# RWKV-7 keys stage: a slab's blocks and bonus sums written inside the next slab's projection, four small copies a slab on ScalarE

## The chip, the cores and the metric

The kernel runs on one core of a Trainium2 chip. The metric is the device time of one launch in microseconds (us). The engines of the core are TensorE (PE in the profile, its weight loads PEld), VectorE (DVE), ScalarE (ACT), GpSimd (POOL) and SyncE (SP), which here issues the DMAs. The engines run their own instruction lists in order and wait for one another by semaphores.

## What is computed

One inference step of two decoder layers, an RWKV-7 layer and a native sparse attention layer, for 512 prompt tokens and 8 sequences of 4 sample tokens. The change is in the RWKV-7 layer. Cut to what matters, the reference computes there:

```
r, k, v, z = einsum(stack([xr, xk, xv, xg]), w_rkvz)
a = sigmoid(a0 + (xa @ a1) @ a2)
kk = heads(k * k_k);  kk = kk / max(sqrt(sum(kk * kk, -1)), 1e-12)
k = k * (1 + (a - 1) * k_a)
y, S = wkv_scan(S0, r, decay, k, v, -kk, kk * a)
bonus = (sum(r * k * r_k, -1) * v)
```

The scan is done in chunks of 64 tokens. For each chunk and head the kernel needs the strictly lower (nilpotent) 64 x 64 block of products between the vectors kk * a and -kk, scaled by the decay, and later its inverse. The bonus needs one sum a head and token of r * k * r_k.

## The kernel before

The 544 tokens (512 of the prompt, 32 of the samples) lie along the free dimension in two halves of 272 columns (256 prompt tokens and 16 sample columns each); the 1024 channels are eight slabs of 128 partitions, two heads a slab. A projection of a slab (products, L317) is eight steps over the input channels, each of three products (high x high, high x low, low x high parts) for two halves: 48 matmuls at L325. Its result lies in a PSUM tile of tag pp.

The stage around the change is keys (L914). For each slab m from 0 to 7 it loads and splits the weights, projects the keys (L964; in the profile "pp<-t"), and then makes the scaled vectors: squares and a copy of k on ScalarE (L966, L968); the cumulated decay (L973, VectorE) and its exponentials (L979, L980, ScalarE); the sums a head of the squares (head_sums, L953, into PSUM tags s0 and s1) with L987, L989 and L990 on ScalarE behind them; the normalised kk (L992 to L995, VectorE and ScalarE); k2 (L998, VectorE) and b = kk * a (L1000, GpSimd); and the tiles ar (L1005, L1007 on VectorE) and bk (L1006 on GpSimd, L1008 on VectorE), which go to DRAM by four DMAs of SP.

Then come the two steps that the change moves. n_blocks (L927) takes a PSUM tile of tag pr, fills it with 16 matmuls of 64 x 64 blocks (L932; the profile shows 32 entries), masks it into NTt[m] on VectorE (L935) and sends it to DRAM by four DMAs (L940). The bonus part multiplies r, r_k and k2 into rk (L1016, VectorE), sums it a head in two halves (head_sums again, L953, each half in a tile of tag pr) and copies each half to bss on ScalarE (L1022). The tag pr has two buffers, the tag bs three, and the tiles upx, upi, ukkn, uar and ubk one each.

Between them stand three small copies of sample columns, 128 x 32 each, on GpSimd: of kkn, b and k2 into arS and bkS (L1017 to L1019). A fourth, of the sigmoid of the decay into sgS, stands at L971. All four go through the helper samp (L463), whose GpSimd copy is L468 and whose ScalarE copy is L466.

At the end of a slab after(m) (L615) does some steps of the inversion of the first four slabs' blocks (IV: 4, 6 and 6 steps after slabs 4, 5 and 6) and projects values (VS: one slab after each of slabs 2 to 6, three after slab 7; in the profile "pp<-x", with L608 and L612 behind it). value(m) uses bss[m].

The program order is not the order on the engines. The framework's scheduler makes each engine's list: it plays the program through with a model of the instructions' times and takes, of those that the model holds ready, the one that stands first in the program. A tile gets its buffer in the same play. The block tc.issue_after(x) adds an edge that keeps each instruction written in it behind x on the engine of x.

Of the kernel before, what the change touches and what calls it, by code (L numbers as in the profile page):

```python
# [11 lines left out]
AF = mybir.ActivationFunctionType  # L12
# [6 lines left out]
KT = 8  # L19
NT = 544  # L20
HN = 272
HP = 256
# [201 lines left out]
class K:  # L224
# [152 lines left out]
    @staticmethod  # L377
    def h2(t):
        return t.rearrange("p (h n) -> p h n", h=2)
# [534 lines left out]
    def keys(self, Xk, R, out, SG, AA, NTt, PC, arS, bkS, sgS, samp, dAR, dBK, ND, after):  # L914

        nc, I, h2 = self.nc, self.I, self.h2
        ident, gmask = self.C("ident"), self.C("gmask")
        WE = self.WE
        omk = self.c0("omk", (128, 8))
        sums = self.sums.bitcast(F32)  # L920
        reset = self.t("rst")
        nc.sync.dma_start(reset, I["reset"])
        nc.vector.tensor_scalar(omk, self.vec[:, VI["ka"]], -1.0, 1.0, op0=OP.mult, op1=OP.add)
        nkk = self.c0("nkk", (128, 8))
        nc.vector.tensor_scalar(nkk, self.vec[:, VI["kk"]], -1.0, None, op0=OP.mult)

        def n_blocks(p, ar, bk):  # L927
            g, i = divmod(p, 4)
            pw = self.t("pr", (128, 8, 64))
            for c in range(8):  # L930
                for r, par in PARS:
                    nc.tensor.matmul(pw[r, c, :], bk[r, 1, c, :], ar[r, c, 0, :],  # L932
                                     start=True, stop=True)
            t = NTt[p]
            nc.vector.tensor_tensor(t, pw, gmask[:, None, 0:64].to_broadcast([128, 8, 64]), OP.mult)  # L935
            for par in range(2):
                for b in range(2):
                    r = slice(par * 64 + b * 32, par * 64 + b * 32 + 32)
                    j = b * 64 + par * 32 + i * 8
                    nc.sync.dma_start(ND[g][j:j + 8].rearrange("c s t -> s c t"), t[r, :, b * 32:b * 32 + 32])  # L940

        def chunks(t):
            return t.rearrange("p (h c) n -> p h c n", h=2)

        def pv(t):
            return h2(t)[:, :, :HP].rearrange("p h (c n) -> p h c n", c=4)

        def head_sums(x, tags):

            out = []  # L950
            for h in range(2):
                ps = self.t(tags[h], (128, 512))
                nc.tensor.matmul(ps[:, :HN], sums, x[:, h * HN:(h + 1) * HN], start=True, stop=True)  # L953
                out.append(ps)
            return out

        for m in range(KT):
            g, i = divmod(m, 4)
            NTt.append(self.t("p", (128, 8, 64)))
            if PLAN["TN"]:  # L960

                nc.gpsimd.memset(NTt[m][:, 0, 0:1], 0.0)
            w = self.weight(I["rkvz"][1, m], 128, WE["WK"][m])
            pt = self.project(w, Xk)  # L964
            sq = self.t("d")
            nc.scalar.activation(h2(sq), pt[:, :, :HN], AF.Square, scale=self.V("kk", m))  # L966
            kr = self.t("d")
            nc.scalar.activation(h2(kr), pt[:, :, :HN], AF.Copy)  # L968

            sg, aa = SG[m], AA[m]  # L970
            samp(sgS[:, m], h2(sg)[:, :, HP:HN], nc.gpsimd)  # L971
            cs = sg
            nc.vector.tensor_tensor_scan(cs, reset, sg, 0.0, OP.mult, OP.add)  # L973
            csv = pv(cs)
            px = self.t("upx", (128, 8, 65))
            nc.gpsimd.memset(px[:, :, 0:1], 1.0)
            pi = self.t("upi", (128, 8, 64))
            with self.tc.issue_after(self.loaded.ins):
                nc.scalar.activation(chunks(px)[:, :, :, 1:65], csv, AF.Exp, scale=-DEC)  # L979
                nc.scalar.activation(chunks(pi), csv, AF.Exp, scale=DEC)  # L980
            nc.gpsimd.tensor_copy(PC[:, m], px[:, :, 64])


            ln = self.t("d")
            s2 = sq
            for h, ps in enumerate(head_sums(sq, ("s0", "s1"))):
                nc.scalar.activation(h2(s2)[:, h], ps[:, :HN], AF.Relu, bias=self.C("nfloor"))  # L987
            with self.tc.issue_after(self.loaded.ins):
                nc.scalar.activation(ln, s2, AF.Ln, scale=float(2 ** 20), bias=self.C("floor"))  # L989
            nc.scalar.activation(ln, ln, AF.Exp, scale=-0.5, bias=self.C("l2"))  # L990
            kkn = self.t("ukkn")
            nc.vector.scalar_tensor_tensor(kkn, kr, nkk[:, m:m + 1], ln, op0=OP.mult, op1=OP.mult)  # L992
            nc.scalar.activation(ln, ln, AF.Square, scale=math.sqrt(0.5))
            nc.vector.scalar_tensor_tensor(ln, s2, 1e-24, ln, op0=OP.add, op1=OP.mult)
            nc.vector.scalar_tensor_tensor(kkn, ln, 1.5, kkn, op0=OP.subtract, op1=OP.mult)  # L995
            nc.scalar.activation(cs, aa, AF.Identity, scale=self.V("ka", m), bias=omk[:, m:m + 1])
            k2 = kr
            nc.vector.tensor_tensor(k2, kr, cs, OP.mult)  # L998
            b = aa
            nc.gpsimd.tensor_tensor(b, kkn, aa, OP.mult)  # L1000
            ar = self.t("uar", (128, 8, 2, 64))
            bk = self.t("ubk", (128, 2, 8, 64))
            ar4 = ar.rearrange("p (h c) x n -> p h c x n", h=2)
            kp, bp = (chunks(bk[:, x]) for x in range(2))
            nc.vector.scalar_tensor_tensor(ar4[:, :, :, 0, :], pv(kkn), -1.0, chunks(px)[:, :, :, 0:64], op0=OP.mult, op1=OP.mult)  # L1005
            nc.gpsimd.tensor_tensor(bp, pv(b), chunks(pi), OP.mult)  # L1006
            nc.vector.tensor_tensor(ar4[:, :, :, 1, :], pv(R[m]), chunks(px)[:, :, :, 1:65], OP.mult)  # L1007
            nc.vector.tensor_tensor(kp, pv(k2), chunks(pi), OP.mult)  # L1008
            nc.sync.dma_start(dAR[g][:, i], ar.rearrange("p c x n -> p c (x n)"))

            nc.sync.dma_start(dBK[g][0:64, i].rearrange("p x c n -> p (x c n)"), bk[0:64].rearrange("p x c n -> p (x c n)"))
            for x in range(2):
                nc.sync.dma_start(dBK[g][64:128, i, 1 - x].rearrange("p c n -> p (c n)"), bk[64:128, x].rearrange("p c n -> p (c n)"))
            n_blocks(m, ar, bk)
            rk = ln
            nc.vector.scalar_tensor_tensor(rk, R[m], self.V("rk", m), k2, op0=OP.mult, op1=OP.mult)  # L1016
            samp(arS[:, m, 0], h2(kkn)[:, :, HP:HN], nc.gpsimd)  # L1017
            samp(bkS[:, m, 1], h2(b)[:, :, HP:HN], nc.gpsimd)
            samp(bkS[:, m, 0], h2(k2)[:, :, HP:HN], nc.gpsimd)  # L1019
            bss = self.t("bs")  # L1020
            for h, ps in enumerate(head_sums(rk, ("pr", "pr"))):
                nc.scalar.activation(h2(bss)[:, h], ps[:, :HN], AF.Copy)  # L1022
            out.append(bss)
            after(m)

    def invert(self, g, ND, out):
# [1072 lines left out]
```

## Time and profile before

| | before |
|---|---|
| median of 3 runs | 1048.05 us |
| runs | 1044.62 to 1048.57 us |
| the profiled execution | 1046.29 us |
| its span, first to last instruction | 1044.5 us |
| mean granted TensorE clock | 0.965 |
| keys stage, from the first keys projections to the last blocks | about 128 to 270 us of the span |

The profile is one execution. A row of the timeline has the start in us, the duration in us, the engine, the line, the operation, the tile written and those read, the shapes and how many instructions were merged; in brackets how long the engine had been idle before it and what ended that. A row of the waits has the waiting instruction, what it waited for, the total in us, how many times and the longest. A row of a line's instructions has the minimum, median and maximum duration in ns.

### The profile page before, as it was taken

What the parts mean: (1) busy time and instruction counts of PE and PEld (TensorE: products, weight loads), DVE (VectorE), ACT (ScalarE), POOL (GpSimd) and SP (SyncE); (2) the same over time, 40 slices, a digit from 0 to 9 for tenths busy, and PEclk for the clock granted to TensorE, in tenths of its full rate; (3) what the DMA queues carried; (4) which work ended last, traced back from release to release, by engine and by line L of the source; (5) the groups of instructions that cost most, each with busy time, mean ns of one, the idle gap of its engine ahead of it and who ended that gap; (6) DMA issues with size and microseconds to landing.
All of it is one profiled execution on the core that took longest, in us unless ns stands there. A gap on an engine that the chain in (4) does not pass through costs nothing.

```text
span 1044.5 us, 24599 instructions
## 1 busy us (share of the span) xinstructions
PE 971.7 (93%) x9429; PEld 827.5 (79%) x9429; DVE 641.8 (61%) x1468; ACT 546.8 (52%) x1294; POOL 466.4 (45%) x575
## 2 busy tenths in 40 slices
PE   5799998989889989999898799999999998998998
PEld 4799997979777868888778798998667766795876
DVE  3798578798386533556966624655674467528455
ACT  4357686555444235435544635546674466556342
POOL 5913557755830453322222555654344354244430
PEclk8799998999899989999999999999999999998999
DMA  5685425648554454645594633232534421428443
GB/s 184 196 260 203 165 86 160 194 136 225 191 151 120 138 166 136 205 134 125 147 251 146 205 109 114 79 117 81 145 86 124 103 80 51 132 79 260 155 133 108
DMA packets 149448, 153.54 MB, mean 147 GB/s; under 512 B 52946, under 2 KB 99570, under 8 KB 149074
## 3 DMA queue, kind: packets, MB, share of 16 engines
q1 hardware_dynamic: 149330, 151.97, 48.4%
q8 instruction: 74, 1.21, 0.5%
q14 instruction: 44, 0.36, 0.1%
HBM read 111.33 MB, written 43.93 MB: 149 GB/s over the span
## 4 chain that ended last, share of the span: by engine, by line
PE 54%; DVE 8%; DMA 5%; ACT 4%; issue 2%; POOL 2%; SPq 0%; DVEq 0%; POOLq 0%; ACTq 0%
PE ph L325 24%; PE pq L1721 3%; PE pw L1796 3%; PE pq L1780 3%; PE pr L1142 2%; DMA d<-dram 2%; PE ph L2010 1%; DVE l L287 1%; DMA w<-in_nwo 1%; PE ph L360 1%; DVE tmp L1044 1%; PE s L1176 1%; PE pw L1793 1%; DMA w<-in_wo 1%; ACT l L286 1%
## 5 line engine op out<-in xcount | busy, mean ns | idle before, releaser
L325 PE MATMUL ph<-x,l 128*128 128x272 f32 x2448 | 362.4, 299 | 8.9 <-DVE l L287 2.5
L325 PEld LDWEIGHTS ph<-x,l 128*128 128x128 f32 x2448 | 324.2, 192 | 44.8 <-issue 22.6
L287 POOL TENSOR_TENSOR l<-w,l 128x512 fp32r<-128x512 f32 (+2 forms) x118 | 155.4, 1329 | 145.5 <-ACT l L286 132.2
L286 ACT ACTIVATE l<-w 128x512 fp32r<-128x512 f32 (+2 forms) x160 | 93.2, 613 | 106.1 <-PE ph L325 38.6
L325 PE MATMUL pp<-x,l 128*128 128x272 f32 x768 | 112.0, 300 | 5.7 <-POOL l L287 5.7
L325 PEld LDWEIGHTS pp<-x,l 128*128 128x128 f32 x768 | 104.4, 196 | 8.3 <-POOL l L287 5.9
L1736 ACT ACTIVATE a<-a,st 128x512 f32<-128x512 f32 (+3 forms) x128 | 70.5, 553 | 30.2 <-DVE st L1729 30.0
L1729 DVE CUSTOM_DVE_ANT_0 a<-pq,tb 128x512 f32<-128x512 f32 (+3 forms) x128 | 56.8, 484 | 19.6 <-PE pq L1721 19.4
L1783 ACT ACTIVATE h<-pq 128x512 f32<-128x512 f32 x60 | 35.5, 592 | 50.2 <-PE pq L1780 50.1
L1486 DVE TENSOR_TENSOR d<-ph,RS 128x272 f32<-128x272 f32 x56 | 24.3, 438 | 60.9 <-PE ph L325 56.7
L1721 PE MATMUL pq<-p,p 64*128 64x512 f32 (+6 forms) x256 | 55.2, 497 | 1.3 <-DVE st L1729 1.3
L325 PE MATMUL pp<-t,l 128*128 128x272 f32 x384 | 54.9, 295 | 0.0
L1780 PE MATMUL pq<-cst,a 128*128 128x128 f32 x320 | 50.8, 279 | 3.7 <-ACT h L1783 1.8
L1756 DVE TENSOR_SCALAR a<-a,st 128x128 f32<-128x128 f32 (+3 forms) x112 | 53.1, 535 | 0.7
L325 PEld LDWEIGHTS pp<-t,l 128*128 128x128 f32 x384 | 50.9, 190 | 0.9
L1780 PEld LDWEIGHTS pq<-cst,a 128*128 128x128 f32 x320 | 35.9, 140 | 18.4 <-issue 11.2
L287 POOL TENSOR_TENSOR d<-d,d 128x544 fp32r<-128x544 f32 (+2 forms) x21 | 28.6, 1363 | 45.6 <-ACT d L286 32.6
L1796 PE MATMUL pw<-h,p 128*64 128x256 f32 x320 | 47.1, 392 | 1.1 <-ACT h L1783 0.6
L287 DVE TENSOR_TENSOR l<-w,l 128x512 fp32r<-128x512 f32 x42 | 37.2, 898 | 16.1 <-ACT l L286 16.0
L656 POOL TENSOR_TENSOR d<-d,d 128x544 f32<-128x544 f32 x8 | 11.1, 1383 | 58.6 <-ACT d L374 58.6
L1749 POOL TENSOR_TENSOR cc<-cc,st 128x64 f32<-128x64 f32 x32 | 11.6, 363 | 56.1 <-DVE st L1746 35.9
L794 POOL TENSOR_TENSOR RS<-RS,d 128x272 f32<-128x272 f32 x14 | 12.9, 923 | 44.1 <-ACT d L793 40.5
(414 smaller groups left out, 1980.9 us busy)
## 6 DMA issues: line engine op xcount, KB each, us to landing
w<-in_rkvz SPq DMA_DIRECT2D x64, 256.0 KB, 2.9
d<-dram SPq DMA_DIRECT2D x54, 272.0 KB, 4.5
w<-in_win SPq DMA_DIRECT2D x56, 256.0 KB, 2.9
dram<-d SPq DMA_DIRECT2D x48, 272.0 KB, 2.5
ab<-dram SPq DMA_DIRECT2D x32, 256.0 KB, 3.7
p<-in_xT SPq DMA_DIRECT2D x16, 272.0 KB, 4.3
tb<-dram SPq DMA_DIRECT2D x16, 264.0 KB, 5.3
dram<-uar SPq DMA_DIRECT2D x8, 512.0 KB, 3.6
```

Source lines behind the costliest of these rows:

```text
L286: nc.scalar.activation(hi, raw, AF.Copy)
L287: (eng or nc.gpsimd).tensor_tensor(lo, raw, hi.bitcast(F32), OP.subtract)
L325: nc.tensor.matmul((pt[h][:m, :HN] if split else pt[:m, h, :HN]), a[:, k, :m], b[:, h * HN:(h + 1) * HN], start=(k == 0 and n == 0), stop= ...
L1142: nc.tensor.matmul(pg[par][r, i], BK[r, i, par], AR[r, i].rearrange("p a b -> p (a b)"), start=True, stop=True)
L1486: self.nc.vector.tensor_tensor(o, p, r, OP.mult)
L1721: nc.tensor.matmul(p[:, par, 0:hi - lo], Q[2 * k + m][r, tk], kk[par][r, lo:hi], start=True, stop=True)
L1729: nc.vector.tensor_tensor_reduce(out=P[par][j], in0=p[:, par, :n], in1=TB[k][:, g, o:o + n], scale=-1.0, scalar=3.0e38, op0=OP.add, op1=OP ...
L1736: nc.scalar.activation(P[par][j], P[par][j], AF.Exp, scale=-1.0, bias=st[:, 0, g, j + 1:j + 2], accum_out=st[:, 1, g, j + 1:j + 2])
L1756: (nc.gpsimd if e == "p" else nc.vector).tensor_scalar(pj, pj, rr, None, op0=OP.mult)
L1780: nc.tensor.transpose(pt[:, g % 2, g // 2], PB[g][j][:, c * 128:c * 128 + 128], ident)
L1783: nc.scalar.activation(w, pt, AF.Copy)
L1796: nc.tensor.matmul(po[r], v, W[x][:, par], start=False, stop=(x == ns - 1), skip_group_check=True)
```

## The change

n_blocks(m), head_sums(rk) of slab m and the two copies behind them are no longer written at the end of slab m. They are written, by the new function follow, after the seventh of the eight steps of slab m+1's projection, with an edge that keeps their matmuls behind the last matmul written so far, the 42nd of 48. Slab 7's stand at its own end as before. The four sample copies of each slab go to ScalarE.

```
+        def follow(held):
+            m, ar, bk, rk = held
+            n_blocks(m, ar, bk)
+            bss = self.t("bs")
+            for h, ps in enumerate(head_sums(rk, ("pr", "pr"))):
+                nc.scalar.activation(h2(bss)[:, h], ps[:, :HN], AF.Copy)
+            out.append(bss)
+
+        late = None
         for m in range(KT):
...
-            pt = self.project(w, Xk)
+            pt = self.PP()
+            for step, _ in enumerate(self.products(pt, w, Xk)):
+                if step == KT - 2 and late:
+                    with self.tc.issue_after(next(i for i in reversed(nc.cur_bb.bb.instructions) if i.engine == mybir.EngineType.PE)):
+                        follow(late)
...
-            samp(sgS[:, m], h2(sg)[:, :, HP:HN], nc.gpsimd)
+            samp(sgS[:, m], h2(sg)[:, :, HP:HN], nc.scalar)
...
-            n_blocks(m, ar, bk)
             rk = ln
             nc.vector.scalar_tensor_tensor(rk, R[m], self.V("rk", m), k2, op0=OP.mult, op1=OP.mult)
-            samp(arS[:, m, 0], h2(kkn)[:, :, HP:HN], nc.gpsimd)
-            samp(bkS[:, m, 1], h2(b)[:, :, HP:HN], nc.gpsimd)
-            samp(bkS[:, m, 0], h2(k2)[:, :, HP:HN], nc.gpsimd)
-            bss = self.t("bs")
-            for h, ps in enumerate(head_sums(rk, ("pr", "pr"))):
-                nc.scalar.activation(h2(bss)[:, h], ps[:, :HN], AF.Copy)
-            out.append(bss)
+            samp(arS[:, m, 0], h2(kkn)[:, :, HP:HN], nc.scalar)
+            samp(bkS[:, m, 1], h2(b)[:, :, HP:HN], nc.scalar)
+            samp(bkS[:, m, 0], h2(k2)[:, :, HP:HN], nc.scalar)
+            late = (m, ar, bk, rk)
+            if m == KT - 1:
+                follow(late)
             after(m)
```

## The prediction

> **What bounds the kernel now.** I read the page first, for the whole, then the table of busy time by stretch for the keys stage, then TensorE's waits in that stage, then the order of instructions engine by engine.
>
> ```profile
> span 1044.5 us, 24599 instructions
> ...
> PE 971.7 (93%) x9429; PEld 827.5 (79%) x9429; DVE 641.8 (61%) x1468; ACT 546.8 (52%) x1294; POOL 466.4 (45%) x575
> ```
>
> TensorE is busy 93% of the span, so only what it idles, or runs at a lower clock, can be won: 1044.5 - 971.7 = 72.8 us in all. The change touches the keys stage, which I cut at the starts of the blocks' matmuls (L932), so that each stretch is about one slab. Columns: the stretch, its length, then busy time and instructions of PE, PEld, DVE, ACT and POOL, TensorE's granted clock, DMA.
>
> ```profile
> 166.99:179.69 12.70, 9.89 (x74) 9.07 (x74) 11.94 (x11) 6.92 (x13) 10.54 (x13) 0.73 0.61 184
> ...
> 211.00:229.34 18.34, 14.19 (x131) 13.52 (x130) 17.86 (x31) 8.54 (x17) 7.70 (x11) 1.00 0.41 132
> 229.34:247.52 18.18, 18.18 (x145) 17.18 (x145) 17.19 (x21) 9.60 (x17) 12.37 (x15) 0.91 0.71 209
> ...
> sum 132.00, PE 120.56 PEld 114.13 DVE 107.41 ACT 80.13 POOL 82.60; mean PE 13.39 PEld 12.68 DVE 11.93 ACT 8.90 POOL 9.18
> ```
>
> The nine stretches together (138 to 270 us) are 132.00 us, of which TensorE is busy 120.56: it idles 11.44 us here. VectorE is nearly full in the two late slabs (17.86 of 18.34, 17.19 of 18.18), ScalarE has half its time free. Two stretches show less than full clock. What TensorE waits for in the same window (total, times, longest):
>
> ```profile
> PE pr L953 <- DVE p L935: 4.7, 3, 1.9
> PE pr L932 <- POOL ubk L1006: 3.9, 3, 2.3
> PE pr L953 <- ACT bs L1022: 2.8, 1, 2.8
> ```
>
> These three are the whole 11.4. Only the second is a wait of the blocks for their operands. The other two are the bonus sums waiting for a PSUM buffer of tag pr: there are two, the blocks take one and the two halves of the sums two more, so the third of each slab needs L935 or L1022 to have emptied one. The change adds no buffer.
>
> **Part one: blocks and sums inside the next projection.** The program order isn't the order on the engines: they run a list that the framework's scheduler made by when its own time model held each instruction ready. So the first question is where L932 stands now. TensorE's own order around slabs 4 and 5 (pp<-t is a keys projection, pp<-x a values projection):
>
> ```profile
> 199.32 6.14 PE L325 MATMUL pp<-t,l 128*128 128x272 f32 x48
> ...
> 205.31 4.46 PE L325 MATMUL pp<-x,l 128*128 128x272 f32 x34
> 209.61 1.08 PE L953 MATMUL s<-d,sums 128*128 128x272 f32 x4
> 210.32 0.74 PE L325 MATMUL pp<-x,l 128*128 128x272 f32 x3
> 211.00 1.15 PE L932 MATMUL pr<-uar,ubk 64*64 64x64 f32 x32
> ```
> ```profile
> 217.41 0.72 PE L953 MATMUL pr<-d,sums 128*128 128x272 f32 x2 [1.84 <-DVE p L935]
> 217.77 4.98 PE L325 MATMUL pp<-t,l 128*128 128x272 f32 x37
> 222.59 4.44 PE L325 MATMUL pp<-x,l 128*128 128x272 f32 x34
> 229.34 1.15 PE L932 MATMUL pr<-uar,ubk 64*64 64x64 f32 x32 [2.31 <-POOL ubk L1006]
> ```
>
> The first fence is slab 4: its blocks run at 211.00, after all 48 matmuls of slab 5's projection (199.32) and 37 of a values projection. The second is slab 5: blocks at 229.34, after slab 6's projection (217.77) and 34 of the next values. The other slabs that have a successor show the same order, the first two with still more projection ahead. So the added edge, "not before the 42nd of 48 matmuls of the next projection", holds already, in these two by over 5 us (from 199.32 + 6.14 to 211.00, from 217.77 + 4.98 to 229.34). What changes is rank: the blocks and sums now rank behind the first 42 matmuls and behind after(m). But what they push aside in both fences is the values projection of after(m+1), which follows them in the old program and in the new. I count 0 removed and 0 added matmuls, and 0 us for TensorE's order. The same holds for what moves along: L935 on VectorE, two L1022 on ScalarE and four L940 on the SP queue a slab. They rank now behind after(m)'s inversion steps, values weights and bonus store and behind the next slab's weight loads, but wait for L932 anyhow, which comes after those.
>
> The uncertainty of this zero: above, if L935 or L1022 slide back further, TensorE stands longer at the third pr buffer; below, if the new rank lets more matmuls go ahead of L932, some of the 3.9 us disappear.
>
> **Part two: four copies a slab from GpSimd to ScalarE.** The rows of line 468 (min/median/max ns) and of the same copy on ScalarE, which the kernel already does once a slab from PSUM:
>
> ```profile
> L468 POOL COPY v<-d x8: 209/686/709, 150.1 to 256.0; 128x32 f32<-128x32 f32 x8
> L468 POOL COPY v<-ukkn x8: 209/708/713, 153.3 to 260.7; 128x32 f32<-128x32 f32 x8
> L468 POOL COPY v<-p x8: 203/670/856, 157.4 to 262.6; 128x32 f32<-128x32 f32 x8
> ...
> L466 ACT ACTIVATE v<-pp x8: 188/192/257, 72.9 to 130.0; 128x32 f32<-128x32 f32 x8
> ```
>
> GpSimd loses 8 x (0.686 + 0.708 + 0.670) = 16.5 us of busy time and the eight sigmoid copies. ScalarE gains 32 x 0.192 = 6.1 us. Neither is the bound, so only the chain counts. One of the copies (v<-ukkn, L1017) stands on GpSimd between L1000 and L1006, whose result L932 waits for. GpSimd, then VectorE, in slab 4:
>
> ```profile
> 205.64 1.76 POOL L1000 TENSOR_TENSOR p<-ukkn,p 128x544 f32<-128x544 f32 x1
> 207.34 0.71 POOL L468 COPY v<-ukkn 128x32 f32<-128x32 f32 x1
> 207.98 0.11 POOL L976 MEMSET upx<- 128x8 f32 x1
> ...
> 208.43 1.29 POOL L1006 TENSOR_TENSOR ubk<-p,upi 128x512 f32<-128x512 f32 x1
> ```
> ```profile
> 206.09 1.89 DVE L1016 SCALAR_TENSOR_TENSOR d<-p,vec,d 128x544 f32<-128x544 f32 x1
> ```
>
> It looks like 0.71 us for the taking. But the copy ends at 207.34 + 0.71 = 208.05, just after VectorE's L1016 ends (206.09 + 1.89 = 207.98). Alone the copy takes 0.21 (its minimum): for 0.5 us it stood behind L1016. Without it the next GpSimd operation stands behind L1016 instead, and L1006 comes forward by 208.05 - 207.98 = 0.07, say 0.1 us. I take 0.1 x 8 = 0.8 us; the upper bound, the whole copy off every slab's chain, is 0.71 x 8 = 5.7 us.
>
> The Trainium skill speaks against that upper bound (SBUF — State Buffer, "Who interferes with whom"): a VectorE instruction with two SBUF inputs and a GpSimd instruction that reads SBUF exclude each other for a whole instruction, while ScalarE never waits on anyone. By this rule the gain is the 0.8 and not the 5.7, and the trace agrees with 0.71 beside a VectorE operation against 0.21 without.
>
> On ScalarE's side the copies fall where it waits (L979 below, 4.72 us idle) or where it doesn't. A copy in a gap costs nothing, one inside the run from the sums' L987 to L990 costs its 0.19 us. I take one of four as felt: 8 x 0.19 = 1.5 us at most if each is passed on, and half of that, 0.8 us, since in slab 5 (DVE 17.86 of 18.34) VectorE is late anyhow. Sum: 0 - 0.8 + 0.8 = 0. The profiled execution took 1046.29 us (span 1044.5), below the median of 1048.05 and inside the three runs (1044.62 to 1048.57). I forecast **1046 us**.
>
> **Rivals.** *Faster: the waits on the blocks go.* The scheduler gets shorter GpSimd queues and lower rank for L932, and fills 229.34's wait with more values matmuls. That is worth more than its idle time, because the clock is low after a long wait:
>
> ```profile
> 170.94:172.93 1.99, 1.99 (x7) 1.75 (x8) 1.99 (x2) 0.40 (x1) 1.96 (x2) 0.50 0.82 214
> 172.93:177.20 4.27, 4.27 (x23) 4.23 (x23) 4.24 (x5) 2.26 (x4) 4.15 (x5) 0.60 0.30 99
> ...
> 217.41:222.70 5.29, 5.29 (x40) 5.21 (x41) 5.29 (x7) 0.94 (x2) 2.79 (x4) 1.00 0.16 25
> 229.34:232.41 3.07, 3.07 (x39) 2.57 (x39) 3.04 (x4) 2.13 (x4) 3.07 (x3) 0.76 0.33 95
> 232.41:235.50 3.09, 3.09 (x18) 2.97 (x17) 2.27 (x5) 2.48 (x5) 0.25 (x2) 0.68 0.97 314
> ```
>
> After the wait of 2.31 us the clock is 0.76 and 0.68: 3.07 x 0.24 + 3.09 x 0.32 = 1.7 us lost. After the longest, 2.8 us on L1022, it is 0.50 and 0.60: 1.99 x 0.50 + 4.27 x 0.40 = 2.7 us. After 1.84 us (ended at 217.41) it is 1.00. So the blocks' waits are worth 3.9 + 1.7 = 5.6 us (1040.7), and all three kinds 11.4 + 1.7 + 2.7 = 15.8 us (1030.5). For it: the two long waits are accidents of order that any reshuffle may remove. Against: the ranking against the filler is unchanged, and 7.5 of the 11.4 us are for pr buffers. The Trainium skill (TensorE: Matmul & The Clock Gate, "What's actually happening") gives a full idle window of about 3.4 us as what halves the clock; here 2.31 us are enough for a part and 1.84 us are not, and I go by the rows.
>
> *Slower: a copy blocks ScalarE's queue.* ScalarE runs in order. Its copy of b (L1018) needs L1000 on GpSimd, and behind it may stand L979 and L966 of the next slab:
>
> ```profile
> 206.20 0.63 ACT L979 ACTIVATE upx<-p 128x512 f32<-128x512 f32 x1 [4.72 <-DVE uar L1005]
> ...
> 207.78 0.70 ACT L966 ACTIVATE d<-pp,vec 128x544 f32<-128x544 f32 x1
> ```
>
> L1000 ended at 205.64 + 1.76 = 207.40. A copy placed ahead of L979 would hold ScalarE from 206.20 to 207.40 and 0.19 more: 1.4 us a slab, 7 x 1.4 = 9.8 us in all, 1056 us. The scheduler has to believe L1000 done before L1005 for this, and the slab must pass it on. Since VectorE's share of the period hides some slabs, I hold this for less likely than its rival.
>
> *The added edge binds after all.* If L932 were really issued in its program place, behind the 42nd matmul, TensorE would stand there for L1006: slab 5's projection ended near 205.3, L1006 of slab 4 at 208.43 + 1.29 = 209.72, so 4.4 us a slab, 7 x 4.4 = 31 us, 1077 us, with six matmuls, L966 and the whole next slab's chain queued behind. Against it: the order by readiness that the fences show.
>
> **How the numbers follow.** A difference of 0.5%, about 5.2 us, is what a measurement of this kernel can tell from no change. Forecast (nothing on the path, or a few us either way): 0.52. Faster rival, from 5.6 us saved on: 0.28. ScalarE's queue held, with other bad reshuffles of the pr buffers of about 5.5 us each (2.8 us of wait and 2.7 of clock): 0.17. The edge binding: 0.03. So faster 0.28, same 0.52, slower 0.20. The range leaves out the largest part of the faster case (waits of all kinds gone) and the binding edge: from 1036, which is 10 us saved of the 15.8, to 1056, ScalarE held in every slab.
>
> **What would show it.** Right: L932 still behind the next projection and some 30 values matmuls; TensorE's waits between 138 and 270 us still near 11 us, mainly pr L953; L1006 starting at the end of L1016 in each slab; 32 ScalarE copies near 0.19 us, none with a long wait ahead; the stage as long as before within 3 us. Wrong: L932 running elsewhere, a wait of L932 on L1006 gone or grown, ScalarE idle at L468 or its copies, or a stretch with the clock at 0.7 that is new or gone. If the stage is as long as before and the time still differs, the scheduler reordered a later stage and my reading of the change by its own stage fails.

## The result and the profile after

The changed kernel takes 1061.7 us (1060.99 to 1063.41, 4 runs) against 1046.5 us (1044.62 to 1048.57, 4 runs) before: a ratio of 1.0144, 95% interval 1.0119 to 1.0169. It is slower by 15 us. The forecast was 1046 us with a range from 1036 to 1056; it was wrong.

The page of the changed kernel:

```profile
span 1059.3 us, 24598 instructions
...
PE 967.8 (91%) x9429; PEld 825.6 (78%) x9429; DVE 641.0 (61%) x1468; ACT 550.6 (52%) x1326; POOL 454.7 (43%) x543
```

TensorE does the same 9429 matmuls in 3.9 us less busy time, and the span is 14.8 us longer: what came is idle time. ScalarE has its 32 instructions more, GpSimd 32 fewer. TensorE's waits in the keys stage, 138 to 270 us (in the changed kernel the lines of the slab loop stand 9 to 13 lines lower, L1019 is L1006 of before; n_blocks and head_sums keep their numbers, and the moved copies, L1022 of before, are L962):

```profile
PE pr L953 <- ACT bs L962: 5.3, 2, 3.5
PE pr L953 <- DVE p L935: 5.2, 2, 3.7
PE pr L932 <- POOL ubk L1019: 4.5, 3, 3.1
```

That is 15.0 us against the 11.4 before, of the same three kinds. But this isn't where the 15 us stay. The matmuls of one line that runs through the whole RWKV scan, L1142 before and L1153 after (min/median/max ns, then the first and the last start), before:

```profile
L1142 PE MATMUL pr<-ab,ab x256: 269/269/320, 333.5 to 522.9; 64*64 64x128 f32 x128
```

and after:

```profile
L1153 PE MATMUL pr<-ab,ab x256: 269/269/320, 333.3 to 538.0; 64*64 64x128 f32 x128
```

The first of them starts 0.2 us earlier than before, the last 15.1 us later. So the scan begins on time, and the loss is laid in stages in which the change edits no line. A start on time doesn't mean that nothing is lost by then, since other work may have been put off. So here is what TensorE does by stretch, just ahead of the scan's start and in its middle. Before:

```profile
308.00:333.00 25.00, 23.47 (x403) 16.29 (x399) 15.44 (x20) 10.82 (x29) 3.15 (x3) 1.00 0.59 168
390.00:460.00 70.00, 68.79 (x1181) 60.01 (x1179) 29.95 (x65) 34.66 (x81) 22.10 (x19) 1.00 0.56 171
```

and after, with the one long wait of the first stretch:

```profile
308.00:333.00 25.00, 21.51 (x345) 15.57 (x342) 13.79 (x17) 7.76 (x21) 2.62 (x3) 0.80 0.65 176
390.00:460.00 70.00, 60.19 (x1012) 54.10 (x1012) 27.71 (x59) 27.62 (x64) 19.05 (x16) 0.90 0.45 137
```
```profile
313.80 1.07 PE L1106 MATMUL s<-p,q 64*32 64x32 f32 x32 [3.49 <-DVE p L1097]
```

From 308 to 333 us TensorE idles 3.5 instead of 1.5 us and has 0.80 of the clock, from 390 to 460 us it idles 9.8 instead of 1.2 and has 0.90. The second stretch is where most of the loss lies. Up to 308 us the two executions come out nearly alike: from 128 us on the changed kernel idles 17.5 us instead of 13.2, but loses less to the low clock.

**Where it goes in the second stretch.** TensorE's waits between 385 and 460 us, before:

```profile
PE s L1095 <- ACT p L1098: 1.2, 1, 1.2
```

and after:

```profile
PE s L1087 <- DVE q L1083: 3.9, 1, 3.9
PE ph L360 <- DVE p L284: 3.4, 2, 3.2
PE pr L1153 <- ACT q L1147: 2.2, 1, 2.2
PE pr L1106 <- DVE p L1097: 1.2, 1, 1.2
```

One wait of 1.2 us has become 10.7 us. The first of the new ones shows how. It is the inversion's second group, which comes back from DRAM (q<-dram) to be transposed on VectorE (L1072 before, L1083 after). VectorE and TensorE of the kernel before:

```profile
391.95 0.71 DVE L1072 STREAM_TRANSPOSE q<-q 128x512 f32<-128x512 f32 x1 [2.46 <-DMA q<-dram]
```
```profile
389.02 3.15 PE L325 MATMUL ph<-x,l 128*128 128x272 f32 x24
392.02 0.39 PE L713 MATMUL ph<-d,mean 128*128 128x512 f32 x1
392.25 1.91 PE L325 MATMUL ph<-x,l 128*128 128x272 f32 x14
394.08 1.15 PE L1076 MATMUL s<-q,p 64*64 64x64 f32 x32
```

and of the changed one:

```profile
392.10 0.71 DVE L1083 STREAM_TRANSPOSE q<-q 128x512 f32<-128x512 f32 x1 [3.76 <-DMA q<-dram]
```
```profile
388.41 0.68 PE L1173 MATMUL s<-f,ab 64*64 64x64 f32 x15
392.95 1.65 PE L1087 MATMUL s<-q,p 64*64 64x64 f32 x26 [3.86 <-DVE q L1083]
...
395.94 2.33 PE L325 MATMUL ph<-x,l 128*128 128x272 f32 x12
```

The transfer lands at the same time in both, 391.95 and 392.10. Before, TensorE is busy through it with 38 projection matmuls (L325) that depend on nothing here. After, those stand behind the step that waits, from 395.94. The work and the transfer are the same; only the cover has gone to another place in the list.

The clock then adds to it. These are the two stretches of the changed kernel between 390 and 460 us in which TensorE is granted half its clock; they go with the first two waits:

```profile
390.60:397.40 6.80, 4.45 (x56) 4.26 (x57) 3.69 (x8) 3.28 (x5) 2.17 (x3) 0.50 0.55 142
414.50:421.30 6.80, 5.57 (x99) 4.96 (x100) 1.28 (x2) 2.65 (x8) 3.12 (x4) 0.50 0.26 85
```

Reckoned as half of its time, the work done in them costs 4.45 x 0.50 + 5.57 x 0.50 = 5.0 us. With 9.8 - 1.2 = 8.6 us of idle time that is 13.6 us from 390 to 460 us. From 308 to 333 us the same reckoning gives 2.0 us of idle time and 4.3 us of low clock (8.50 us of work at half clock), 6.3 us. Between the two it is the kernel before that loses 3.2 us more, with a wait of 2.7 us for L286 and 6.8 us at half clock. The sum, 6.3 - 3.2 + 13.6 = 16.7 us, is an estimate from one execution of each; it accounts for the 15.

### The profile page after: what moved, and what is told of

Same layout as the page of the kernel before. It is cut to its first block, busy times and chain, and to the rows that moved or that the text cites. A ratio compares the mean times of both kernels' runs of the same rounds, so it can differ in the third digit from the quotient of the medians.

```text
span 1059.3 us, 24598 instructions
## 1 busy us (share of the span) xinstructions
PE 967.8 (91%) x9429; PEld 825.6 (78%) x9429; DVE 641.0 (61%) x1468; ACT 550.6 (52%) x1326; POOL 454.7 (43%) x543
## 4 chain that ended last, share of the span: by engine, by line
PE 56%; DVE 14%; DMA 10%; ACT 7%; POOL 7%; issue 4%; SPq 2%; DVEq 0%; POOLq 0%; ACTq 0%
PE ph L325 24%; PE pq L1732 3%; PE pw L1807 3%; PE pq L1791 3%; PE pr L1153 2%; DVE l L287 2%; DMA d<-dram 1%; POOL l L287 1%; PE ph L2021 1%; ACT l L286 1%; DMA w<-in_rkvz 1%; DVE d L443 1%; PE pp L325 1%; DMA dram<-d 1%; DMA dram<-ubk 1%
## 5 line engine op out<-in xcount | busy, mean ns | idle before, releaser
L325 PE MATMUL ph<-x,l 128*128 128x272 f32 x2448 | 361.4, 298 | 7.9 <-ACT l L286 1.8
L325 PEld LDWEIGHTS ph<-x,l 128*128 128x128 f32 x2448 | 323.4, 191 | 42.7 <-issue 23.2
L287 POOL TENSOR_TENSOR l<-w,l 128x512 fp32r<-128x512 f32 (+2 forms) x118 | 155.4, 1328 | 161.5 <-ACT l L286 131.5
L286 ACT ACTIVATE l<-w 128x512 fp32r<-128x512 f32 (+2 forms) x160 | 93.4, 612 | 99.4 <-PE ph L325 36.3
L325 PE MATMUL pp<-x,l 128*128 128x272 f32 x768 | 108.3, 295 | 5.5 <-POOL l L287 5.5
L325 PEld LDWEIGHTS pp<-x,l 128*128 128x128 f32 x768 | 101.6, 191 | 7.6 <-POOL l L287 5.7
L325 PE MATMUL pp<-t,l 128*128 128x272 f32 x384 | 55.5, 298 | 0.0
L325 PEld LDWEIGHTS pp<-t,l 128*128 128x128 f32 x384 | 51.6, 194 | 0.8
L1791 PEld LDWEIGHTS pq<-cst,a 128*128 128x128 f32 x320 | 35.9, 140 | 18.7 <-issue 11.4
L287 DVE TENSOR_TENSOR l<-w,l 128x512 fp32r<-128x512 f32 x42 | 33.9, 817 | 20.9 <-ACT l L286 18.9
L287 POOL TENSOR_TENSOR d<-d,d 128x544 fp32r<-128x544 f32 (+2 forms) x21 | 28.2, 1344 | 39.6 <-ACT d L286 27.0
L1153 PE MATMUL pr<-ab,ab 64*64 64x128 f32 x256 | 32.0, 275 | 2.2 <-ACT q L1147 2.2
```

The source lines that it names most:

```text
L286: nc.scalar.activation(hi, raw, AF.Copy)
L287: (eng or nc.gpsimd).tensor_tensor(lo, raw, hi.bitcast(F32), OP.subtract)
L325: nc.tensor.matmul((pt[h][:m, :HN] if split else pt[:m, h, :HN]), a[:, k, :m], b[:, h * HN:(h + 1) * HN], start=(k == 0 and n == 0), stop= ...
L1153: nc.tensor.matmul(pg[par][r, i], BK[r, i, par], AR[r, i].rearrange("p a b -> p (a b)"), start=True, stop=True)
L1791: nc.tensor.transpose(pt[:, g % 2, g // 2], PB[g][j][:, c * 128:c * 128 + 128], ident)
```

## Experiments

Ratios are to the kernel before, run on the same chip beside each kernel, with their 95% intervals. Code is shortened.

**Which half of the change.** The first run makes only the move, with the copies left on GpSimd.

```
+                        follow(late)             (the move and the edge, as in the change)
             samp(..., nc.gpsimd)             (all four copies, as before)
```

> Only the first part of the change: blocks and bonus sums inside the next projection, the four copies on GpSimd as before. The scheduler gives every engine the same list as before. Both theories (reshuffle and blocked queue) put all of the loss on the copies, so both expect the time before: ratio 1.000, within 0.3%. A third theory, that the moved step costs something by itself, would need over 1.005.

1.0013 (0.9987 to 1.0039): no change. The reason is plain when the lists are laid side by side: in the traces all five engines run, instruction for instruction, the lists of the kernel before. The changed kernel differs from this one by the engine of the four copies alone. So the title of the change names two edits, and one of them does nothing: the whole of the 15 us hangs on which engine does 32 copies of 128 x 32.

**The copies, or the order that came with them.** In the traces the lists of the two kernels differ from ahead of the keys stage (about 115 us; SyncE's from 178 us) to 454 us of the trace before and 474 us of the one after, and are the same behind that. To part the copies from the order, the next kernels hold the instructions in a recorded order:

```
+    for engine, names in RECORDED:             # order lists of one of the two kernels
+        for prev, this in zip(names, names[1:]):
+            tc.add_manual_dep(this, prev, NoSync)  # issue order on that engine, no semaphore
```

First three with the copies on ScalarE, where the scheduler places only the copies themselves: every shared instruction in the order of the kernel before; the keys stage and what stands ahead of it in the new order and the rest in the old; the keys stage in the old order and the rest in the new.

> The kernel before with the four copies on ScalarE, and all instructions that it shares with before held in the order of before on every engine (edges that fix issue order only). Theory one, reshuffle: the copies cost nothing themselves and the new order of the other instructions is the whole loss of 15 us; expects within 3 us of before (0.997 to 1.003). Theory two, blocked queue: ScalarE stands at the copies for VectorE's and GpSimd's results (16 us of such waits in the profile after) and holds the instructions behind them; expects most of the loss still there, 8 to 15 us (1.008 to 1.014).

> Copies on ScalarE; the instructions written in the keys stage and before it held in the order of the changed kernel, all written later held in the order of before. Theory one, if the loss is split as the trace shows (the last blocks start 5.8 us later, the end 14.8 us later): 5 to 6 us, about 1052. If the keys stage's delay is absorbed later: within 3 us. Theory two: the whole loss, about 1061, since ScalarE's lists in the keys stage are those of the changed kernel.

> The reverse: copies on ScalarE, the keys stage in the order of before, everything written later in the order of the changed kernel. Theory one: the part of the loss that the trace shows behind the keys stage, 8 to 10 us, about 1056. Theory two: the copies' own waits stay, and the later order matters little: within 3 us of copies_old_order.

1.0064 (1.0039 to 1.0089), 1.0069 (1.0042 to 1.0096) and 1.0207 (1.0183 to 1.0230). With the rest in the old order the loss is about 7 us whichever order the keys stage has; with the rest in the new order it is more than the whole. Of these, 1.0064 and 1.0207 lie in no range that theory one or two gave. They suggested two losses which add up in the changed kernel, 7 us for the copies and 8 for the order. The next run tests this from the other side: the kernel before, copies on GpSimd, held in the order of the changed kernel.

```
+RECORDED = lists of the changed kernel     (on the kernel before; its GpSimd copies not held)
```

> Edit: the kernel before, its 32 sample copies still on GpSimd, but every instruction that it shares with the changed kernel is held in the order that the changed kernel's engines have. Theory A (two losses that add up: the copies standing in ScalarE's queue, about 7 us, and the new order of the rates and low-rank stage, about 8 us): only the second is left, so +6 to +10 us over before, a ratio of 1.006 to 1.010, and the waits for the gates' low-rank weights near 395 to 420 us are there as in the changed kernel. Theory B (the order is the whole loss): +13 to +17 us, 1.012 to 1.016. Theory C (the copies on ScalarE are the whole loss and the order only shows it): within 3 us of before, 0.997 to 1.003.

1.0159 (1.0129 to 1.0189), which is theory B. With none of these copies on ScalarE the order alone (and the buffers that the scheduler hands out along it) costs as much as the whole change. The sum of two losses has fallen: what the copies cost in the old order is not added to what the new order costs.

**The 7 us of the copies in the old order.** Two runs ask what they are. In copies_old_order ScalarE sits idle ahead of the copies (L466), with weight roundings behind them in its queue:

```profile
ACT v L466 <- DVE ukkn L997: 14.6, 5, 4.1
...
ACT v L466 <- POOL p L1002: 3.7, 2, 2.5
ACT v L466 <- DVE d L1000: 3.0, 3, 2.1
```

One kernel puts the chain's copies where their source is ready, the other moves only the copy of the decay.

```
+RECORDED = lists of the kernel before, L466 (v<-ukkn, v<-p, v<-d) put in 0.6 us behind their source's end
```

> Edit: the changed kernel in the order of the kernel before on every engine, as in copies_old_order (1.0064), but the three copies of each slab's chain are put on ScalarE at a place where, by the times of the kernel before, their source has been ready for 0.6 us; there the scheduler had put several of them 2 to 6 us ahead of that time, and weight roundings (L286) behind them. The copies of the gates' sample columns stay where they were. Theory D (ScalarE's queue stands behind a copy whose source isn't ready): most of the 7 us goes, 0.999 to 1.003. Theory E (the time of the 32 copies on ScalarE, 32 x 0.19 = 6 us, is felt wherever they stand): 1.005 to 1.008.

```
-            samp(arS ..), samp(bkS ..), samp(bkS ..) on nc.scalar      (stay on nc.gpsimd)
+RECORDED = lists of the kernel before
```

> Edit: of the four copies a slab only the one of the decay's sample columns (vs<-p) is on ScalarE, the three of the chain stay on GpSimd; every other instruction is in the order of the kernel before. Theory D (the chain's copies block ScalarE's queue): within 2 us of before, 0.998 to 1.002, since this copy's source is ready long before. Theory E (time on ScalarE): a quarter of the 7 us, 1.001 to 1.003. Theory F (the decay's scan on VectorE waits for this copy on ScalarE, and that is the 7 us): 1.005 to 1.008.

1.0044 (1.0018 to 1.0069) and 1.0002 (0.9982 to 1.0022). So the decay's copy costs 2 us at most, and the three of the chain cost some 5 to 7 us. The second run also shows that holding a list by such edges costs nothing that can be told from zero. Put late, ScalarE's idle time ahead of them falls from 21.3 us to 8.0:

```profile
ACT v L466 <- DVE ukkn L997: 4.6, 3, 4.0
ACT v L466 <- DVE d L1000: 3.4, 3, 2.1
```

but 1.0044 lies between what D and E expected, and its interval overlaps that of 1.0064. How much is a blocked queue and how much the copies' own time stays open.

**Which part of the order.** Copies on GpSimd in all of these. The program is cut by instruction number; one part is in the new order, all else in the old. Where two parts meet, the scheduler still chooses. In all of these but the early stretch's one table load of SyncE (relb) also goes out at 14 us instead of 30; no run parts it from the rest, but the first keys projection starts at 126 to 131 us with it and without it.

```
+RECORDED = lists of the kernel before for one part of the instruction numbers,
+           lists of the changed kernel for the other
```

> Edit: the kernel before with its copies on GpSimd; every instruction that stands in the program up to the second chunk group's inversion (about the first 350 us of the trace) is held in the order of the kernel before, every one behind it in the order of the changed kernel. Whole new order: 1.0159. Theory L (the order around 390 to 480 us, where the waits and the low clock of the changed kernel's trace stand, is the loss): +12 to +18 us, 1.011 to 1.017. Theory E (the loss is laid early, by the order of 260 to 350 us, and is only seen later): within 3 us of before, 0.997 to 1.003. Theory S (shared): 1.004 to 1.010 here and in early_stretch_new_order alike.

> Edit: as the one before, the other way round: new order only for the instructions behind the keys stage and ahead of the second chunk group's inversion (about 260 to 350 us); keys stage and all behind in the order of the kernel before. Theory L: 0.997 to 1.003. Theory E: 1.011 to 1.017.

> Edit: new order only for the instructions up to the end of the keys stage, everything behind in the order of the kernel before, copies on GpSimd. Both theories expect 0.997 to 1.003; with the copies on ScalarE the new and the old order of this stage measured alike (1.0069 and 1.0064). Should the last blocks' delay of 5.8 us, which the trace of the changed kernel shows at 263 us, last to the end, it would be 1.005.

> Edit: as late_stretch_new_order, but the new order begins only behind the second chunk group's first inversion and merge steps, so that these stand in the old order too; the gates' low-rank products, the next slabs' scan steps and the loads of this stretch are in the new order. Theory L1 (the waits for the inversion's and merge's results, which the new order calls for earlier, are the loss): 0.998 to 1.004. Theory L2 (what stands behind them, the low-rank products and the scan's steps, is the loss): 1.010 to 1.017.

| new order in | ratio |
|---|---|
| keys stage and ahead (to about 260 us) | 1.0086 (1.0056 to 1.0116) |
| early stretch (260 to 350 us) | 1.0031 (1.0011 to 1.0050) |
| late stretch (behind 350 us) | 1.0168 (1.0146 to 1.0190) |
| of it, last part only (behind the inversion's second group) | 1.0145 (1.0122 to 1.0168) |

Theory L, and L2 of the last run: the last part alone carries a loss as large as the whole. That is not the inversion's wait shown above, which is absent here; this kernel waits 2.5 us for the low-rank weights and 3.1 us for the state's copy instead. And the parts don't add: 1045 us x (0.0086 + 0.0031 + 0.0168) = 29.8 us against 1045 x 0.0159 = 16.6 for the whole order. That an earlier part only delays what a later part would have waited for anyhow would explain it, but no run shows that. The keys stage's new order, of which the changed kernel's trace shows little by 308 us, costs 9 us ahead of the old rest, against the expectation of both theories. One more cut:

```
+RECORDED = as last_part_new_order, new order only for the first half of it (second half of it)
```

> Edit: copies on GpSimd; new order only for the first half of the last part's instructions (second inversion's end, gates' first low-rank products, first scan steps; about 385 to 425 us), all else in the order of the kernel before. Theory P (the loss is laid where the low-rank weights come late, at 395 to 420 us): 1.008 to 1.015. Theory Q (the scan's steps behind, where the wait for the state's copy of 3 to 4.7 us and the low clock at 440 to 480 us stand): 0.998 to 1.005.

> Edit: the other half: new order only for what stands behind that (second low-rank products, next scan steps, output weights; about 425 to 480 us). Theory P: 0.998 to 1.005. Theory Q: 1.008 to 1.015. If neither half loses more than 1.005, the loss comes only of both together.

1.0202 (1.0172 to 1.0232) and 1.0080 (1.0057 to 1.0104). Each half by itself loses more than 0.5%, so P and Q both fall as they were put; the first half alone loses more than both together.

**Single waits.** Five runs mend single waits, the last of them two at once. In the changed kernel SyncE's queue has the two table loads (L1350, L1354) ahead of the gates' low-rank weights (L303, L682), for which VectorE's L284 and then TensorE's L360 wait. SyncE's queue:

```profile
408.25 0.33 SPq L1350 DMA_DIRECT2D l<-in_onehot  x1
408.68 0.38 SPq L1354 DMA_DIRECT2D l<-in_bneg  x1
409.15 0.38 SPq L303 DMA_DIRECT2D d<-in_lg  x1
409.62 0.38 SPq L682 DMA_DIRECT2D d<-in_lg2b  x1
```

Before, the same two low-rank loads went out ahead of the tables:

```profile
392.06 0.39 SPq L303 DMA_DIRECT2D d<-in_lg  x1
...
396.60 0.31 SPq L1339 DMA_DIRECT2D l<-in_onehot  x1
```

It looked like the cause: 409.15 - 392.06 = 17 us late, behind table loads that wait for a free buffer. The first run puts the weights ahead, the second the tables far behind.

```
 SyncE's list of the changed kernel:
-  l<-in_onehot, l<-in_bneg, d<-in_lg, d<-in_lg2b
+  d<-in_lg, d<-in_lg2b, l<-in_onehot, l<-in_bneg
```

> Edit: the changed kernel held in its own order on all engines, but for two transfers: on SyncE's queue the first loads of the gates' low-rank weights (L303 and L682, d<-in_lg and d<-in_lg2b) stand ahead of the two table loads (l<-in_onehot, l<-in_bneg) as they do in the kernel before, where in the changed kernel they stand behind them and behind a wait of 13.7 us for a free l buffer. Theory A1 (that queue's head is what the later stage loses): 4 to 8 us shorter than the changed kernel, a ratio to before of 1.006 to 1.010, and VectorE's idle time of 5.0 us ahead of L284 goes. Theory A2 (the later stage loses by the order of inversion steps and merge on TensorE and VectorE, and the loads only arrive late beside it): within 3 us of the changed kernel, 1.011 to 1.017.

```
-  l<-in_onehot, l<-in_bneg, d<-in_lg, d<-in_lg2b, dram<-d .. (10 more)
+  d<-in_lg, d<-in_lg2b, dram<-d .. (10 more), l<-in_onehot, l<-in_bneg      (copies on GpSimd)
```

> Edit: gpsimd_new_order (1.0159), but on SyncE's queue the two table loads (l<-in_onehot, l<-in_bneg), which wait for a free l buffer, stand some fourteen places later, just ahead of the stores of the table that they fill, so that neither the low-rank weights nor the stores and loads of the gates' rows stand behind that wait. Theory H (the blocked head of SyncE's queue causes the later loss): 1.003 to 1.010. Theory N (it only comes beside it; TensorE and VectorE wait for each other by their new order all the same): 1.013 to 1.019.

1.0168 (1.0120 to 1.0217) and 1.0139 (1.0114 to 1.0165): theories A2 and N. TensorE's waits from 385 to 460 us with the tables late:

```profile
PE s L1078 <- DVE q L1074: 3.3, 1, 3.3
PE pr L1144 <- ACT q L1138: 2.7, 1, 2.7
PE ph L360 <- POOL p L687: 1.4, 1, 1.4
PE ph L360 <- POOL p L287: 0.9, 1, 0.9
```

L360 no longer waits for L284, but for the next operand of the same product on GpSimd, 2.3 us instead of the 3.0 of gpsimd_new_order. The blocked queue was real and mending it was worth little.

The other wait that the last part's kernels share is that of L1144 (L1142 of before) for the state's copy on ScalarE. In second_half_of_last_part it is the one long wait that the kernel before hasn't. ScalarE there:

```profile
435.18 0.63 ACT L286 ACTIVATE l<-w 128x512 fp32r<-128x512 f32 x1 [3.79 <-DMA w<-in_wo]
...
436.26 0.58 ACT L1138 ACTIVATE q<-pr 128x512 f32<-128x512 f32 x1
```

The copy (L1138) stands behind the rounding of an output weight (L286) whose transfer hasn't landed. The next three kernels move the two roundings behind the copies, in the whole new order, in the half, and in the changed kernel itself (there with the tables late as well).

```
 ScalarE's list:
-  L286 (w<-in_wo), L372, L1138, L286 (w<-in_wo), L373, L1138, L374
+  L372, L1138, L373, L1138, L374, L286 (w<-in_wo), L286 (w<-in_wo)
```

> Edit: gpsimd_new_order (1.0159, wait for the state copy 4.0 us), but on ScalarE the two roundings of the output weights (L286) that wait for a transfer stand behind the two state copies (L1138) and the gates' activations. Theory W (this wait of 4 us and the low clock behind it, some 6 us more, are the greater part of the loss): 1.004 to 1.009. Theory X (the wait goes, but TensorE then waits for the next late thing): 1.012 to 1.018.

> Edit: the same move in second_half_of_last_part (1.0080, wait for the state copy 4.3 us, the only long wait that the kernel before hasn't). Theory W: 0.997 to 1.003. Theory X: 1.006 to 1.010.

> Edit: the changed kernel, copies on ScalarE, in its own order, but for the two roundings behind the state copies and the two table loads just ahead of their stores. Theory W: 1.002 to 1.009 against the 1.0144 of the changed kernel. Theory X: 1.011 to 1.016.

1.0128 (1.0104 to 1.0151), 1.0065 (1.0042 to 1.0088) and 1.0157 (1.0131 to 1.0184): theory X three times. The intervals overlap those without the edit (1.0159, 1.0080, 1.0144). The wait did go, but see what took its place in state_copy_first_second_half, on TensorE, then on VectorE:

```profile
440.32 2.18 PE L360 MATMUL ph<-p,p 128*128 128x272 f32 x8 [3.99 <-DVE p L284]
```
```profile
438.11 0.69 DVE L287 TENSOR_TENSOR l<-w,l 128x512 fp32r<-128x512 f32 x1 [4.54 <-ACT l L286]
...
439.85 0.42 DVE L284 CAST p<-d 128x512 fp32r<-128x512 f32 x1
```

The second half of the split of the same weight (L287) heads VectorE's queue, and L284 stands behind it. A wait of 4.32 us for L1138 became one of 3.99 us for L284: the same late transfer, met one engine later.

What is shown: the order of the lists is enough for the whole loss with no copy moved (1.0159), and so is the order of the last part alone (1.0145). What is argued from the traces: the chain's steps of this stretch come ahead of work that used to cover their transfers. What stays open is the least set of moves that would win it back; SyncE's order of the whole stretch (both pairs of low-rank weights and the output weights together) wasn't tried. No version here beats the kernel before.

## Why the prediction was wrong, point by point

*Part one, zero.* Right, and exactly so: the lists of moved_only are those of before. The added edge held already, as the two fences of slabs 4 and 5 said. The binding edge (0.03) is out.

*What bounds the kernel.* Two small misreadings: of the nine stretches three and not two show less than full clock (262.69 to 270.00 us has 0.90), and ScalarE is busy for 80.13 of 132.00 us, so less than half its time is free. Nothing in the forecast hangs on either.

*Part two, GpSimd.* Right in its mechanism where it looked. In slab 4 of the changed kernel L1019 (L1006) starts at the end of L1028 (L1016), 207.62 + 1.88 = 209.50. VectorE, then GpSimd:

```profile
207.62 1.88 DVE L1028 SCALAR_TENSOR_TENSOR d<-p,vec,d 128x544 f32<-128x544 f32 x1
```
```profile
209.52 1.26 POOL L1019 TENSOR_TENSOR ubk<-p,upi 128x512 f32<-128x512 f32 x1
```

Before, it started 208.43 - 207.98 = 0.45 us behind the end of L1016, now 0.02: brought forward by 0.4 us, more than the 0.07 foreseen, since other small GpSimd instructions stood there too, and less than the copy's 0.71. It still waits for the end of the VectorE instruction, as the rule of the Trainium skill (SBUF — State Buffer, "Who interferes with whom") has it. But the sign asked for, L1006 at the end of L1016 "in each slab", is there in slabs 3 and 4, nearly in slab 6, and not in the other five, where L1019 starts behind other instructions, such as GpSimd's roundings L287.

*Part two, ScalarE.* The 32 copies run at medians of 0.224 to 0.276 us, not 0.192: 8 x (0.276 + 0.228 + 0.230 + 0.224) = 7.7 us. That is a small miss. The larger one is the 0.8 us felt: in the old order the copies cost about 7 us (1.0064). In the changed kernel ScalarE waits at them:

```profile
  DVE ukkn L1008: 16.1, 6
  DVE d L1011: 1.8, 1
  POOL upx L989: 0.5, 1
```

18.4 us of idle time ahead of the copies. The rival "a copy blocks ScalarE's queue" foresaw such waits, with the wrong copy (kkn, waiting for L1008, before b), and its 9.8 us stand beside the 7 us of copies_old_order; how much of these is a blocked queue stays open, as said above. Even this rival isn't what makes the 15 us: the new order with the copies left on GpSimd costs as much.

*The step that failed* is the sum 0 - 0.8 + 0.8 = 0. It was made over the keys stage alone, "neither is the bound, so only the chain counts", with every list behind the stage taken as it was, so the new lists of the later stages were put at nothing without a reason. The runs put them at 1.0159 by themselves, about 16.6 us, and at 1.0145 for the last part alone. The prediction had the premise at hand: in part one it said that the engines run a list which the scheduler makes by when its own model holds each instruction ready. It then asked of part one where the list puts the moved instructions, and didn't ask of part two what the list does when 32 instructions change their engine and so their time. Its last sentence named the case, "the stage is as long as before and the time still differs" (here the stage's last blocks start 6.6 us later, at 270.2 instead of 263.6, and yet the scan behind it begins on time), but gave it neither a chance nor a price, while the faster rival, which also rests on a reshuffle, got 0.28.

*The chances.* A reshuffle was treated as a coin. Of the seven orders measured here with the copies on GpSimd, the whole one and six parts, all seven are slower, by 3 to 21 us, and none is faster. Only the whole one was drawn by the scheduler; the six are mixtures of it with the old one, so this is one draw and not seven. It bears out that the waits of the old order were not accidents that any new order may remove; how a further draw would fall, no run shows.

## What to carry to other kernels

Where a scheduler makes the engines' lists, an edit that changes an instruction's engine draws the order anew for everything behind it that is still in reach, here some 350 us. Compare the built lists before reading any stage: if they are equal there is nothing to predict, and if they differ far from the edit, the loss will be looked for in the wrong place. For a kernel whose order is already good, give a new draw its own chance, on the slow side too; this case has one such draw, and it lost 15 us. And a long wait in a list is seldom one fault: before mending it, see what stands next in each queue behind the same late transfer.

## What the runs showed of the hardware

The granted clock falls behind a single wait and takes some time to come back. Cut where it changes, the clock in these traces is either full or half; a value between, like the 0.76 and 0.68 of the prediction, is the mean of a stretch with a change in it. Before, then after, behind the wait of 3.49 us that ends at 313.80:

```profile
231.00:234.40 3.40, 3.40 (x13) 2.94 (x12) 3.33 (x5) 2.19 (x5) 1.66 (x3) 0.50 0.78 219
```
```profile
312.10:322.30 10.20, 8.50 (x140) 6.65 (x140) 2.33 (x4) 1.82 (x6) 0.00 (x0) 0.50 1.00 275
```

and in second_half_of_last_part, around the wait of 4.32 us that ends at 436.89:

```profile
435.70:449.30 13.60, 12.41 (x110) 11.58 (x110) 6.96 (x14) 3.23 (x7) 4.78 (x4) 0.50 0.28 81
449.30:452.70 3.40, 3.40 (x50) 2.89 (x48) 0.42 (x1) 2.19 (x7) 0.00 (x0) 1.00 0.81 238
```

These 13.6 us at half clock cost 12.41 x 0.50 = 6.2 us, more than the wait itself. In the changed kernel the wait of 3.49 us brought 10.2 us at half clock, which cost 4.3 us; those of 3.86 and 3.16 us brought 6.8 us each, which cost 2.2 and 2.8. So the price of a wait isn't fixed by its length.
